# Encoder layer in split fp32: row and block sums of the second MLP product placed elsewhere, and the q and k evictions at the highest priority on VectorE

## The chip, the cores and the metric

One core of one Trainium2 chip. The metric is the device time of one launch in microseconds (us), the median of several runs. A core has five engines that run side by side, each with its own queue of instructions that it takes strictly in order: TensorE (PE in the profile), VectorE (DVE), ScalarE (ACT), GpSimd (POOL) and SyncE (SP), which here computes nothing and issues nearly all transfers between HBM and SBUF. Matrix products land in PSUM, in eight banks of 128 x 512 fp32.

## The reference, cut to what matters

The input is x of 1024 rows (positions) by 1024 columns. All is fp32.

```
h = rmsnorm(x, g_mix);  z = h @ w_in;  q, k, v, ... = split(z)
x = x + concat([gated linear attention(q, k, v, ...), spatial gating(...)]) @ w_out
h = rmsnorm(x, g_mlp)
x = x + square(relu(h @ w1)) @ w2          # w1: 1024 x 4096, w2: 4096 x 1024
out = rmsnorm(x, g_final)                  # x * rsqrt(mean(x*x) + eps) * g
```

## The kernel before, in words

**Precision.** TensorE multiplies rounded values, so each operand tile is split in two: `split` rounds a 128 x 512 tile on ScalarE (the cast, L124) and takes the rest on VectorE (the "lo split", L125). A product then takes three matmuls, hi x hi, hi x lo and lo x hi. Both halves live in tiles named xa, of which there are 16: `put2` takes two for each split operand, so splits can run 8 operands ahead of TensorE, which is two pairs of the passes 1 to 3 below.

**The MLP by blocks.** Both MLP products follow a Strassen-Winograd scheme, with 7 block products instead of 8. The first product (`mlp1`, 16 steps p, one for each pair of hidden tiles) computes h = relu(..)^2 by blocks and stores to HBM (tiles hA, hS) the blocks A11, A12, A22 and the sums S1 to S4 that the second product needs. The norm in front of the MLP is not applied to x2 (the x after attention): its row factor is left out of the hidden values and comes back at the end, where out = (x2 + r2 * y), and r2 = 1 / (mean(x2*x2) + eps) for each row. x2 itself is kept in HBM (x2n, natural order) and read again for this.

**The second product** runs in four passes over the same 16 pairs p:
- pass 1: X += A11.B11, Y += A12.B21. At its end the X banks are copied to U on ScalarE, and C11 = Y + U on VectorE (L566).
- pass 2: X += S1.T1, Y += S2.T2, with T1 = B12 - B11 and T2 = B22 - T1 taken on VectorE (`sub2`, L563). At its end u5 = X (ScalarE), U += Y and u5 += U (VectorE).
- pass 3: Y += A22.T4 first, then X += S3.T3, with T4 = B21 - T2 and T3 = T2 - B11.
- pass 4: X += S4.B22; the last three pairs are done bank by bank, so that the rows of a bank can be finished while the next one runs.

X and Y are four banks each (pf and pg in the profile, which lists a bank by its pool). A pass begins to write a bank as soon as the adds or copies that read it at the end of the pass before are done. One block product of a pair (`product2`) is 12 matmuls, a pair of passes 1 to 3 has 24, a pair of pass 4 has 12.

**Row work.** `row_load` brings a half row block of x2 (128 x 512) into a tile (qk for rows 4 to 7, a part of V for rows 0 to 3) and squares it on ScalarE (L872) for r2; `row_add` (L883) adds r2 times one of the blocks C11, U, u5, X, Y; `sq` squares the sums for the last norm; `finish` applies factor and gain gB: a GpSimd multiply (L921) and a ScalarE scaling (L922) for the left half, one VectorE instruction (L924) for the right half.

**Order.** The order on an engine is fixed when the kernel is built, by a list scheduler that models the engines and prefers instructions of higher priority (`tc.high_priority(offset=..)`; HP and HPE are 400, HP2 is 160). On TensorE the program's order is kept. Loads of the four passes are chained in program order by `load2`; which buffers they rotate through is set by `streams` (hidden blocks) and `raws` (weights). A load waits on SP until its buffer is free, and what stands behind it on SP waits too.

**q and k.** Early in the kernel the projections of q and k are taken out of PSUM by `qk_evac` (a VectorE multiply by the row factor, L296, and a ScalarE copy), while the stages of the attention before them (`st_cum`, L335 to L349; `st_kv`, L404 and L410) use the same engines.

Of the kernel before, what the change touches and what calls it, by code (L numbers as in the profile page):

```python
# [7 lines left out]
F32 = mybir.dt.float32  # L8
# [23 lines left out]
def tile_encoder(  # L32
# [110 lines left out]
    one("pad", [P, 32])  # L143
# [145 lines left out]
    def qk_evac(dst, i):  # L289
        def done(ps, hf):  # L290
            r = R[:, hf * 512 : hf * 512 + 512]
            for j in range(2):
# [3 lines left out]
                nc.vector.tensor_tensor(out=t[own], in0=ps[own], in1=r[own], op=ALU.mult)  # L296
# [340 lines left out]


# [54 lines left out]
    def mlp1(p):  # L693
# [36 lines left out]
        nc.scalar.copy(out=h12, in_=b)  # L730
# [4 lines left out]
        keep("S4", p, s4)  # L735

    mlp1(0)
    x2_natural(order[-1])
    for p in range(1, NPAIR):
        mlp1(p)  # L740
# [3 lines left out]
    streams = [("la", 3)] * 3 + [("qin", 2)] * 2 + [("kin", 2)] * 2 + [("kd", 1)]  # L744
    sn = [0, None]

    def load2(t, src):

        ins = nc.sync.dma_start(out=t, in_=src)
        if sn[1] is not None:  # L750
            tc.add_manual_dep(
                ins.ins,
                sn[1].ins.name,
                mybir.DependencyInfo(mybir.DependencyClass.NoSync, mybir.DependencyReason.DATA),
                reason="load order",
            )
        sn[1] = ins
# [299 lines left out]
```

## Time and profile before

| | |
|---|---|
| median of 3 runs | 1052.75 us (1051.12 to 1054.19) |
| the profiled execution | 1054.3 us, of which 1052.5 from its first to its last instruction |
| busy: PE, DVE, ACT, POOL | 1022.5 (97%), 700.7 (67%), 473.4 (45%), 98.2 (9%) us |
| stages (read from the timeline) | projections and mixers 0 to 316, W_out to 414, first MLP product to 716, pass 1 to 803.0, pass 2 to 895.8, pass 3 to 990.7, pass 4 to 1044.8, tail to 1052.5 |

All times are of the slowest (here the only) core. A busy TensorE is not one at its peak: its share counts a matmul that runs at half clock as busy too. Since TensorE is busy nearly throughout, the time is TensorE's work, plus its waits, plus what its clock loses. "Granted clock" is the share of full speed (2.4 GHz; the other level is 1.2 GHz) that the chip gave TensorE in a stretch.

### The profile page before, as it was taken

The page shows a single profiled execution, that of the slowest core. Times are in us where ns is not written, and L with a number is a line of the kernel's source. Part 1 is how long each engine was busy: PE and PEld are TensorE (multiplying, and loading weights), DVE is VectorE, ACT ScalarE, POOL GpSimd, SP SyncE. Part 2 cuts the span into 40 slices and gives each one's busy share as a digit, 9 for nine tenths or more (in the row PEclk, how much of TensorE's full clock was granted, in tenths as well). Part 3 has the DMA queues.
Part 4 walks back from the last instruction along what each step waited for, and adds up shares of the span by engine and source line. Part 5 has one row for each costly group of instructions (what it writes and reads, how often), then busy time and mean ns, then how long its engine had stood idle before and what let it go on. Part 6 is the DMA issues. An engine that isn't in the chain of part 4 may idle for free. (4 is left out here: it accounts for less than half of the span.)

```text
span 1052.5 us, 14294 instructions
## 1 busy us (share of the span) xinstructions
PE 1022.5 (97%) x5014; PEld 832.1 (79%) x5014; DVE 700.7 (67%) x1172; ACT 473.4 (45%) x903; POOL 98.2 (9%) x116
## 2 busy tenths in 40 slices
PE   9999999999999999999999999999999999899977
PEld 7887778777878888888888888888887887687855
DVE  6247867666664557887776776756457767657784
ACT  7534626455454545433333333334444444345563
POOL 1001423323221000000000000000000000000241
PEclk9999999999999999999999999999999999999989
DMA  9322111111112544554353443339764555464532
GB/s 317 137 76 65 41 51 50 31 31 31 51 40 93 156 124 138 171 183 148 128 184 129 156 171 124 140 140 329 233 208 161 188 171 161 122 198 155 164 112 80
DMA packets 84119, 141.78 MB, mean 135 GB/s; under 512 B 8784, under 2 KB 17744, under 8 KB 84048
## 3 DMA queue, kind: packets, MB, share of 16 engines
q1 hardware_dynamic: 82896, 138.79, 40.2%
q10 hardware_dynamic: 1152, 2.10, 0.5%
q8 instruction: 39, 0.64, 0.2%
q14 instruction: 32, 0.26, 0.1%
HBM read 103.10 MB, written 37.75 MB: 134 GB/s over the span
## 5 line engine op out<-in xcount | busy, mean ns | idle before, releaser
L106 PE MATMUL pg<-xa,xa 128*128 128x512 f32 x768 | 189.5, 397 | 15.4 <-DVE xa L125 9.7
L106 PEld LDWEIGHTS pg<-xa,xa 128*128 128x128 f32 x768 | 145.4, 191 | 51.2 <-DVE xa L125 12.0
L106 PE MATMUL pf<-xa,xa 128*128 128x512 f32 x576 | 139.4, 391 | 0.0
L106 PE MATMUL pf<-xa,wh 128*128 128x512 f32 x336 | 135.9, 405 | 0.0
L106 PE MATMUL pf<-xb,wh 128*128 128x512 f32 x336 | 132.2, 393 | 0.0
L106 PEld LDWEIGHTS pf<-xa,xa 128*128 128x128 f32 x576 | 109.1, 189 | 23.0
L106 PE MATMUL pf<-xa,wl 128*128 128x512 f32 x320 | 125.9, 393 | 0.0
L106 PE MATMUL pf<-V,xa 128*128 128x512 f32 x336 | 91.7, 389 | 0.0
L124 ACT CAST xa<-xb 128x512 fp32r<-128x512 f32 x76 | 47.1, 621 | 98.0 <-PE pf L106 74.7
L125 DVE TENSOR_TENSOR xa<-xb,xa 128x512 fp32r<-128x512 f32 x76 | 52.1, 688 | 55.7 <-ACT xa L124 55.6
L125 DVE TENSOR_TENSOR wl<-wr,wh 128x512 fp32r<-128x512 f32 x63 | 48.9, 776 | 50.3 <-ACT wh L124 50.0
L106 PEld LDWEIGHTS pf<-xa,wh 128*128 128x128 f32 x336 | 63.9, 190 | 14.2 <-issue 1.4
L106 PEld LDWEIGHTS pf<-V,xa 128*128 128x128 f32 x336 | 63.1, 188 | 13.1
L106 PEld LDWEIGHTS pf<-xb,wh 128*128 128x128 f32 x336 | 63.8, 190 | 12.2
L106 PEld LDWEIGHTS pf<-xa,wl 128*128 128x128 f32 x320 | 60.7, 190 | 13.3
L913 POOL TENSOR_SCALAR r<-r 128x1 f32<-128x1 f32 x8 | 3.3, 416 | 680.0 <-ACT tmp L911 679.5
L124 ACT CAST wh<-wr 128x512 fp32r<-128x512 f32 x63 | 38.8, 616 | 60.4 <-PE pf L106 55.1
L124 ACT CAST xa<-k 128x512 fp32r<-128x512 f32 x49 | 30.5, 623 | 78.3 <-PE pf L106 75.5
L106 PE MATMUL pf<-xb,xa 128*128 128x512 f32 x192 | 53.9, 389 | 0.0
L106 PE MATMUL pf<-qk,xa 128*128 128x512 f32 x176 | 52.9, 389 | 0.0
L124 ACT CAST xa<-la 128x512 fp32r<-128x512 f32 x42 | 26.1, 621 | 49.6 <-PE pg L106 30.0
L125 DVE TENSOR_TENSOR xa<-la,xa 128x512 fp32r<-128x512 f32 x42 | 30.0, 713 | 27.4 <-ACT xa L124 27.4
(290 smaller groups left out, 1887.2 us busy)
## 6 DMA issues: line engine op xcount, KB each, us to landing
k<-w SPq DMA_DIRECT2D x64, 256.0 KB, 2.9
hA<-kn SPq DMA_DIRECT2D x32, 256.0 KB, 2.9
hS<-wr SPq DMA_DIRECT2D x32, 256.0 KB, 3.4
la<-hS SPq DMA_DIRECT2D x26, 256.0 KB, 2.7
qk<-xn SPq DMA_DIRECT2D x16, 256.0 KB, 5.4
wr<-wsv SPq DMA_DIRECT2D x16, 256.0 KB, 2.5
wr<-wo SPq DMA_DIRECT2D x16, 256.0 KB, 2.6
x2n<-tmp SPq DMA_DIRECT2D x16, 256.0 KB, 3.9
```

The source lines that it names most:

```text
L106: nc.tensor.matmul(out=o, lhsT=lhsT, rhs=rhs, start=start, stop=stop, skip_group_check=more)
L124: nc.scalar.copy(out=hi, in_=src)
L125: nc.vector.tensor_tensor(out=lo, in0=src, in1=hi.bitcast(F32), op=ALU.subtract)
L913: nc.gpsimd.tensor_scalar(out=r[:, 4:5], in0=r[:, 0:1], scalar1=EPS, scalar2=None, op0=ALU.add)
```

## The change

It consists of these parts.

1. The L296 multiply of `qk_evac` is put at the highest priority.
2. The squares of x2 for r2 leave passes 3 and 4. Eight new loads of a whole row block (128 x 1024, into tile R) and eight ScalarE squares stand in the first MLP product instead, one in each of its steps p = 2 to 9, ordered behind the step's last PSUM copy. r2 follows at p = 10 by two small VectorE instructions.
3. The hidden loads of passes 1 and 2 rotate through 16 buffers instead of 8 (the 8 qk tiles are added), and the weight loads after p = 3 no longer use qk.
4. B11 of pairs 0 and 1 is kept in R from pass 1 on; its two reloads in pass 2 go.
5. `sub2` puts each subtraction behind the lo split that was made 8 operands earlier, so that VectorE no longer reaches a subtraction long before it is needed. The subtractions T3 move with this from pass 2 into pass 3.
6. Additions to rows 4 to 7 move from the end of pass 3 to its pairs 2 to 5, those to rows 0 to 3 from pass 4 to pairs 9 to 12 of pass 3, with their loads; there the left halves of rows 0 to 3 are multiplied by gB as well (VectorE).
7. gB is loaded in pass 3, pair 2, instead of before pass 1.
8. `finish`: for rows 4 to 7 the left half is done by one VectorE instruction (L933 of the kernel after) in place of GpSimd's and ScalarE's, for rows 0 to 3 only ScalarE's scaling is left.

```diff
 def split(src, hi, lo, scale=None):
-            nc.vector.tensor_tensor(out=lo, in0=src, in1=hi.bitcast(F32), op=ALU.subtract)
+            return nc.vector.tensor_tensor(out=lo, in0=src, in1=hi.bitcast(F32), op=ALU.subtract)
 def qk_evac(dst, i):
-                nc.vector.tensor_tensor(out=t[own], in0=ps[own], in1=r[own], op=ALU.mult)
+                with tc.high_priority(offset=HP):
+                    nc.vector.tensor_tensor(out=t[own], in0=ps[own], in1=r[own], op=ALU.mult)
+    def in_order(ins, after):
+        if after is not None:
+            tc.add_manual_dep(ins.ins, after.ins.name, ...NoSync..., reason="order of use")
+        return ins
+    def row_square(t, after):
+        r = sb("R", 1, [P, D])
+        nc.sync.dma_start(out=r, in_=x2n[t])
+        in_order(nc.scalar.activation(out=r, in_=r, func=AF.Square, accum_out=r2[:, t : t + 1]), after)
     for p in range(1, NPAIR):
-        mlp1(p)
+        last = mlp1(p)
+        if 2 <= p < 2 + NT:
+            row_square(p - 2, last)
+        if p == 2 + NT:
+            nc.vector.tensor_scalar(out=r2, in0=r2, scalar1=1.0 / D, scalar2=EPS, op0=ALU.mult, op1=ALU.add)
+            nc.vector.reciprocal(out=r2, in_=r2)
-    streams = [("la", 3)] * 3 + [("qin", 2)] * 2 + [("kin", 2)] * 2 + [("kd", 1)]
+    streams = [("la", 3), ("qin", 2), ("qk", 8), ("kin", 2), ("la", 3), ("qk", 8)] + [("la", 3), ("qin", 2), ("qk", 8), ("kin", 2), ("kd", 1), ("qk", 8)]
 def put2(src):
-            split(src, a, b)
+            loq.append(split(src, a, b))
 def sub2(out, a, b):
-            sub(out, a, b)
+            in_order(nc.vector.tensor_tensor(out=out, in0=a, in1=b, op=ALU.subtract), loq[-8])
     # pass 1
-            raws = [("qk", 8)] * 8 + [("wr", 2), ("tmp", 2), ("sg", 2), ("kn", 2)] * 2
+            raws = [("wr", 2), ("tmp", 2), ("sg", 2), ("kn", 2)] * 2
     # pass 2
-        if p < 2:
-            B11[p] = w2_load(2 * p, 0, big[0][:, p])
     # pass 3
+    streams = [("la", 3), ("qin", 2), ("kin", 2), ("la", 3), ("qin", 2), ("kin", 2), ("la", 3), ("kd", 1)]
-        if p >= 8 and p % 2 == 0:
-            row_load(4 + (p - 8) // 2)
-        if p == NPAIR - 1:
-            row_scale(4)
-            for tt in range(4):
-                row_add(4 + tt, 0, U[tt])
-                row_add(4 + tt, 1, u5[tt])
+        if p == 2:
+            gB = sb("R", 1, [P, D])
+            load2(gB, gfin.broadcast_to([P, D]))
+        if 2 <= p < 6:
+            t = 2 + p
+            row_load(t)
+            row_add(t, 0, U[t - 4])
+            row_add(t, 1, u5[t - 4])
+        if 9 <= p < 13:
+            t = p - 9
+            row_load(t)
+            row_add(t, 0, C11[t])
+            sq(r0[t], 0, rows[t, 0], 512)
+            row_add(t, 1, u5[t])
+            nc.vector.tensor_tensor(out=rows[t, 0], in0=rows[t, 0], in1=gB[:, 0:512], op=ALU.mult)
 def finish(t, r):
-        left_eng.tensor_tensor(out=left, in0=left, in1=gB[:, 0:512], op=ALU.mult)
-        tc.keep_in_program_order(nc.scalar.activation(out=left, in_=left, func=AF.Copy, scale=s))
+        if t < 4:
+            tc.keep_in_program_order(nc.scalar.activation(out=left, in_=left, func=AF.Copy, scale=s))
+        else:
+            nc.vector.scalar_tensor_tensor(out=left, in0=left, scalar=s, in1=gB[:, 0:512], op0=ALU.mult, op1=ALU.mult)
     # pass 4
-        if p % 2 == 0 and p < 8:
-            row_load(p // 2)
-        if p == 8:
-            row_scale(0)
-            for tt in range(4):
-                row_add(tt, 0, C11[tt])
-                sq(r0[tt], 0, rows[tt, 0], 512)
-                row_add(tt, 1, u5[tt])
```

TensorE's order is the same in both kernels. What moves stands on VectorE, ScalarE and SP. Three places on VectorE follow; a row is its number, the line, the operation, output<-inputs with buffer numbers, and the tile's shape. Lines of the kernel after are one to some more than before: L297 answers to L296, L350 to L349, L567 to L566, L799 to L563, L882 to L883.

The first is at the second half of the third attention head (projection of k), before and then after. Here the qk tiles are what `qk_evac` writes, the X tiles the attention's states, kin the keys that TensorE waits for.

```order
211 L341 TENSOR_TENSOR sm_1697<-sm_1697 128x8
212 L296 TENSOR_TENSOR qk_1727<-pf_1593,R_496 64x512
213 L410 SCALAR_TENSOR_TENSOR X_1392<-X_1392,sm_1448 64x128
214 L296 TENSOR_TENSOR qk_1730<-pf_1593,R_496 64x512
215 L346 SCALAR_TENSOR_TENSOR qin_1703<-qin_1703,qk_1159 128x512
216 L125 TENSOR_TENSOR wl_1943<-wr_1940,wh_1942 128x512
217 L410 SCALAR_TENSOR_TENSOR X_1392<-X_1392,sm_1174 64x128
218 L349 TENSOR_TENSOR kin_1702<-kin_1702,qk_1682 128x512
```

```order
209 L342 TENSOR_TENSOR sm_1697<-sm_1697 128x8
210 L411 SCALAR_TENSOR_TENSOR X_1392<-X_1392,sm_1448 64x128
211 L297 TENSOR_TENSOR qk_1727<-pf_1593,R_496 64x512
212 L297 TENSOR_TENSOR qk_1730<-pf_1593,R_496 64x512
213 L411 SCALAR_TENSOR_TENSOR X_1392<-X_1392,sm_1448 64x128
214 L347 SCALAR_TENSOR_TENSOR qin_1703<-qin_1703,qk_1159 128x512
215 L125 TENSOR_TENSOR wl_1943<-wr_1940,wh_1942 128x512
216 L350 TENSOR_TENSOR kin_1702<-kin_1702,qk_1682 128x512
```

The two multiplies stand side by side, and the state update that stood right ahead of kin is gone from there (it follows behind).

The second is the end of pass 2 and the start of pass 3. The adds that read pg are U0 to U3; each must be done before pass 3 writes that bank.

```order
986 L125 TENSOR_TENSOR xa_8116<-V_6575,xa_8115 128x512
987 L125 TENSOR_TENSOR xa_8150<-qin_8143,xa_8149 128x512
988 L566 TENSOR_TENSOR wl_7231<-pg_7255,wl_7231 128x512
989 L563 TENSOR_TENSOR sg_8291<-sg_8291,xb_7472 128x512
990 L566 TENSOR_TENSOR wl_7232<-pg_7256,wl_7232 128x512
991 L125 TENSOR_TENSOR xa_8155<-sg_8147,xa_8154 128x512
992 L566 TENSOR_TENSOR k_7239<-k_7239,wl_7231 128x512
993 L566 TENSOR_TENSOR wl_7233<-pg_7257,wl_7233 128x512
994 L566 TENSOR_TENSOR wh_7234<-pg_7258,wh_7234 128x512
```

```order
972 L799 TENSOR_TENSOR V_6602<-xb_7395,V_6602 128x512
973 L125 TENSOR_TENSOR xa_8175<-kin_8168,xa_8174 128x512
974 L567 TENSOR_TENSOR wl_7258<-pg_7282,wl_7258 128x512
975 L567 TENSOR_TENSOR wl_7259<-pg_7283,wl_7259 128x512
976 L125 TENSOR_TENSOR xa_8180<-sg_8172,xa_8179 128x512
977 L567 TENSOR_TENSOR k_7266<-k_7266,wl_7258 128x512
978 L567 TENSOR_TENSOR wl_7260<-pg_7284,wl_7260 128x512
979 L567 TENSOR_TENSOR k_7267<-k_7267,wl_7259 128x512
980 L567 TENSOR_TENSOR wh_7261<-pg_7285,wh_7261 128x512
```

The subtraction L563 between U0 and U1 (its tile sg is a weight for a pair far ahead) is gone; an add to u5 (tile k) stands between U2 and U3.

The third is pass 4, before and after, from about its middle. V are rows 0 to 3, the qk tiles rows 4 to 7; wh, k are blocks C11 and u5.

```order
1112 L125 TENSOR_TENSOR xa_9164<-xb_7624,xa_9163 128x512
1113 L883 SCALAR_TENSOR_TENSOR V_9000<-wh_7235,r_8085,V_9000 128x512
1114 L883 SCALAR_TENSOR_TENSOR V_9000<-k_7239,r_8085,V_9000 128x512
1115 L883 SCALAR_TENSOR_TENSOR V_9000<-wh_7236,r_8085,V_9000 128x512
1116 L883 SCALAR_TENSOR_TENSOR V_9000<-k_7240,r_8085,V_9000 128x512
1117 L883 SCALAR_TENSOR_TENSOR V_9000<-k_7237,r_8085,V_9000 128x512
1118 L883 SCALAR_TENSOR_TENSOR V_9000<-k_7241,r_8085,V_9000 128x512
1119 L883 SCALAR_TENSOR_TENSOR V_9000<-k_7238,r_8085,V_9000 128x512
1120 L883 SCALAR_TENSOR_TENSOR V_9000<-k_7242,r_8085,V_9000 128x512
1121 L125 TENSOR_TENSOR xa_9182<-la_9179,xa_9181 128x512
```

```order
1107 L125 TENSOR_TENSOR xa_9102<-qin_9099,xa_9101 128x512
1108 L933 SCALAR_TENSOR_TENSOR qk_8266<-qk_8266,r_8953,R_8264 128x512
1109 L937 SCALAR_TENSOR_TENSOR qk_8268<-qk_8268,r_8953,R_8264 128x512
1110 L125 TENSOR_TENSOR xa_9106<-xb_7496,xa_9105 128x512
1111 L933 SCALAR_TENSOR_TENSOR qk_8320<-qk_8320,r_8967,R_8264 128x512
1112 L937 SCALAR_TENSOR_TENSOR qk_8322<-qk_8322,r_8967,R_8264 128x512
1113 L125 TENSOR_TENSOR xa_9124<-kin_9121,xa_9123 128x512
```

The eight additions in a row are gone; the pairs of `finish` instructions stand apart, with a lo split between them.

## Rows read from the trace of the kernel before

**Rows 1.** The page: span, and GB/s in 40 equal slices.

```profile
span 1052.5 us, 14294 instructions
...
GB/s 317 137 76 65 41 51 50 31 31 31 51 40 93 156 124 138 171 183 148 128 184 129 156 171 124 140 140 329 233 208 161 188 171 161 122 198 155 164 112 80
```

**Rows 2.** Windows by stage: length, busy time of each engine, granted clock, DMA share, GB/s.

```profile
414.00:716.00 302.00, 302.00 (x1338) 250.13 (x1338) 221.90 (x347) 108.75 (x193) 0.00 (x0) 1.00 0.46 154
716.00:803.00 87.00, 87.00 (x385) 72.04 (x384) 49.26 (x78) 39.80 (x71) 0.00 (x0) 1.00 0.72 249
803.00:895.80 92.80, 90.16 (x385) 72.47 (x383) 69.50 (x112) 38.55 (x69) 0.00 (x0) 0.98 0.53 170
895.80:990.70 94.90, 89.74 (x385) 73.07 (x385) 62.10 (x101) 41.03 (x80) 0.00 (x0) 0.98 0.53 169
990.70:1044.80 54.10, 46.54 (x193) 36.67 (x192) 39.05 (x56) 32.75 (x78) 20.33 (x27) 0.94 0.23 78
```

**Rows 3.** What PE waited for: us in total, times, longest.

```profile
PE pg L106 <- DVE xa L125: 9.7, 6, 6.6
PE pg L106 <- DVE wl L566: 3.6, 3, 2.0
PE pf L106 <- DVE qk L296: 3.0, 2, 2.6
PE pg L106 <- DVE kin L349: 2.6, 2, 1.3
PE pg L106 <- DVE wh L566: 1.3, 1, 1.3
```

**Rows 4.** Timeline of PE: start, us, what, [idle before <- releaser].

```profile
129.90 0.47 PE L106 MATMUL pf<-wh,xa 128*128 128x512 f32 x1 [2.60 <-DVE qk L296]
...
808.20 0.98 PE L106 MATMUL pg<-xa,xa 128*128 128x512 f32 x3 [1.32 <-DVE wh L566]
...
899.66 0.96 PE L106 MATMUL pg<-xa,xa 128*128 128x512 f32 x3 [1.98 <-DVE wl L566]
...
1021.58 1.65 PE L106 MATMUL pg<-xa,xa 128*128 128x512 f32 x3 [6.61 <-DVE xa L125]
```

**Rows 5.** Window around the end of pass 1, columns as in rows 2.

```profile
789.00:815.00 26.00, 24.42 (x98) 18.90 (x97) 20.27 (x33) 11.14 (x20) 0.00 (x0) 0.93 0.47 156
```

**Rows 6.** Timeline of DVE at the start of pass 2.

```profile
805.18 0.68 DVE L566 TENSOR_TENSOR wh<-pg,wl 128x512 f32<-128x512 f32 x1
806.85 0.69 DVE L563 TENSOR_TENSOR qk<-qk,V 128x512 f32<-128x512 f32 x1 [0.99 <-DMA qk<-w]
807.46 0.68 DVE L566 TENSOR_TENSOR wh<-pg,wl 128x512 f32<-128x512 f32 x1
```

**Rows 7.** Timeline of DVE at the start of pass 3.

```profile
898.31 0.69 DVE L563 TENSOR_TENSOR sg<-sg,xb 128x512 f32<-128x512 f32 x1 [1.72 <-DMA sg<-w]
```

**Rows 8.** Timeline of SP at the end of pass 2.

```profile
895.19 0.42 SPq L749 DMA_DIRECT2D sg<-w  x1
```

**Rows 9.** Timeline of DVE, third attention head.

```profile
188.21 1.02 DVE L410 SCALAR_TENSOR_TENSOR X<-X,sm 64x128 f32<-64x128 f32 x1
```

**Rows 10.** What ACT waited for from 716 to 1045, as in rows 3.

```profile
ACT tmp L872 <- DMA qk<-x2n: 13.6, 4, 4.8
```

**Rows 11.** Timeline of DVE in pass 4.

```profile
1013.15 0.74 DVE L883 SCALAR_TENSOR_TENSOR V<-wh,r,V 128x512 f32<-128x512 f32 x1
1013.81 5.44 DVE L883 SCALAR_TENSOR_TENSOR V<-k,r,V 128x512 f32<-128x512 f32 x5
1019.17 1.75 DVE L125 TENSOR_TENSOR xa<-la,xa 128x512 fp32r<-128x512 f32 x1
```

**Rows 12.** Timeline of POOL in pass 4.

```profile
1016.39 1.64 POOL L921 TENSOR_TENSOR V<-V,R 128x512 f32<-128x512 f32 x1
```

**Rows 13.** Timeline of SP ahead of pass 1.

```profile
711.17 0.32 SPq L749 DMA_DIRECT2D qin<-hA  x1
```

**Rows 14.** Timeline of ACT ahead of pass 1.

```profile
713.85 0.62 ACT L124 CAST xa<-qin 128x512 fp32r<-128x512 f32 x1 [2.54 <-DMA qin<-hA]
```

More of the change, by code (lines that the diff above doesn't have):

```diff
@@ L142, in tile_encoder @@
     ccols = one("cols", [P, 24])
-    one("pad", [P, 32])
+    one("pad", [P, 16])
     warm = sb("tmp", 2)
@@ L636, in tile_encoder @@
             x2_natural(order[n - 1])
+    def in_order(ins, after):
+        if after is not None:
+            tc.add_manual_dep(
+                ins.ins,
+                after.ins.name,
+                mybir.DependencyInfo(mybir.DependencyClass.NoSync, mybir.DependencyReason.DATA),
+                reason="order of use",
+            )
+        return ins
     NPAIR = NFF // 2
@@ L729, in mlp1 @@
         h12 = sb("kn", 2)
-        nc.scalar.copy(out=h12, in_=b)
+        last = nc.scalar.copy(out=h12, in_=b)
         relu2(h12, h12)
@@ L735, in mlp1 @@
         keep("S4", p, s4)
+        return last
+    r2 = one("r2", [P, 8])
+    def row_square(t, after):
+        r = sb("R", 1, [P, D])
+        nc.sync.dma_start(out=r, in_=x2n[t])
+        in_order(nc.scalar.activation(out=r, in_=r, func=AF.Square, accum_out=r2[:, t : t + 1]), after)
     mlp1(0)
@@ L739, in tile_encoder @@
     for p in range(1, NPAIR):
-        mlp1(p)
+        last = mlp1(p)
[4 more added lines that the diff above has]
+            nc.vector.reciprocal(out=r2, in_=r2)
     HP2 = 160
-    streams = [("la", 3)] * 3 + [("qin", 2)] * 2 + [("kin", 2)] * 2 + [("kd", 1)]
-    sn = [0, None]
+    streams = [("la", 3), ("qin", 2), ("qk", 8), ("kin", 2), ("la", 3), ("qk", 8)] + [("la", 3), ("qin", 2), ("qk", 8), ("kin", 2), ("kd", 1), ("qk", 8)]
+    loq = [None]
+    sn = [None]
     def load2(t, src):
[L749 to L757, printed above, removed]
+        sn[0] = in_order(nc.sync.dma_start(out=t, in_=src), sn[0])
         return t
@@ L867, in row_load @@
         for dh in range(2):
-            r = sb("qk", 8) if t >= 4 else rows0[0][:, 2 * t + dh]
-            rows[t, dh] = r
-            load2(r, x2n[t, :, dh * 512 : dh * 512 + 512])
-            junk = sb("tmp", 2, [P, 512], BF16)
-            nc.scalar.activation(out=junk, in_=r, func=AF.Square, accum_out=ss2[:, 8 * dh + t : 8 * dh + t + 1])
-    def row_scale(t0):
-        c = slice(t0, t0 + 4)
-        c2 = slice(8 + t0, 12 + t0)
-        nc.vector.tensor_tensor(out=r2[:, c], in0=ss2[:, c], in1=ss2[:, c2], op=ALU.add)
-        nc.vector.tensor_scalar(out=r2[:, c], in0=r2[:, c], scalar1=1.0 / D, scalar2=EPS, op0=ALU.mult, op1=ALU.add)
-        nc.vector.reciprocal(out=r2[:, c], in_=r2[:, c])
+            rows[t, dh] = sb("qk", 8) if t >= 4 else rows0[0][:, 2 * t + dh]
+            load2(rows[t, dh], x2n[t, :, dh * 512 : dh * 512 + 512])
     def row_add(t, dh, src, sl=slice(0, 512)):
@@ L885, in row_add, with sq @@
         )
+    def sq(r, i, src, n):
+        junk = sb("tmp", 2)
+        nc.scalar.activation(out=junk[:, :n], in_=src, func=AF.Square, scale=D**-0.5, accum_out=r[:, i : i + 1])
+        if i == 0:
+            nc.gpsimd.tensor_scalar(out=r[:, 4:5], in0=r[:, 0:1], scalar1=EPS, scalar2=None, op0=ALU.add)
+        else:
+            nc.gpsimd.tensor_tensor(out=r[:, 4:5], in0=r[:, 4:5], in1=r[:, i : i + 1], op=ALU.add)
     X, Y = [pf() for _ in range(4)], [pg() for _ in range(4)]
     raws = [("wr", 2), ("sg", 2), ("kn", 2)] * 2
+    streams = [("la", 3), ("qin", 2), ("kin", 2), ("la", 3), ("qin", 2), ("kin", 2), ("la", 3), ("kd", 1)]
+    r0 = [sb("r3", 8, [P, 8]) for _ in range(4)]
     for p in range(NPAIR):
@@ L937, in tile_encoder @@
         row_add(t, 1, X[tt])
-        r = sb("r3", 4, [P, 8])
+        r = sb("r3", 8, [P, 8])
         sq(r, 0, rows[t, 0], 512)
         sq(r, 1, rows[t, 1], 512)
-        finish(t, r, nc.gpsimd)
+        finish(t, r)
     X = [pg() for _ in range(4)]
@@ L946, in tile_encoder @@
     tail = []
-    r0 = [sb("r3", 4, [P, 8]) for _ in range(4)]
     for p in range(NPAIR):
@@ L971, in tile_encoder @@
             sq(r0[tt], i + 1, rows[tt, 1][:, c0 : c0 + n], n)
-        finish(tt, r0[tt], nc.gpsimd if tt < 3 else nc.vector)
+        finish(tt, r0[tt])
 def _constants():
```

34 lines of the change are left out of this document (12 added, 22 removed).

## The prediction

> **What bounds the kernel now.** I read the busy shares first: TensorE is busy 97% of the span [rows 1], so only what it waits, and what its clock loses, can be won. The windows by stage say where that is [rows 2]. Pass 1 is the yardstick: 87.0 us with TensorE never idle and the clock at 1.00, so 5.44 us for a pair and 2.72 us for a block product. Pass 2 has the same matmuls and takes 92.8: 5.8 lost. Pass 3 takes 94.9: 7.9 lost. Pass 4 has half of them, 43.5, and takes 54.1: 10.6 lost. The sum is 24.3 us. The first MLP product loses nothing (302.00 of 302.00 busy).
>
> The waits of TensorE give the causes [rows 3]. Of 24.3 us, 14.6 are waits for VectorE with a name: 9.7 for lo splits (L125), 3.6 and 1.3 for the adds that free banks (L566). Much of the rest is the clock: 0.98, 0.98 and 0.94 granted in passes 2, 3 and 4 make 0.02 x 92.8 + 0.02 x 94.9 + 0.06 x 54.1 = 7.0 us. The clock falls around the waits: 0.93 in the 26 us that hold the wait of 1.32 at 808.20, 1.00 in the whole of pass 1 before [rows 2, 4, 5]. So a wait that goes takes its share of the clock's loss with it, and I count a pass by its length. Ahead of the passes, TensorE waits 3.0 us for the q and k multiplies and 2.6 for kin.
>
> The timeline of VectorE shows why it is late though it is busy only two thirds of passes 2 and 3 [rows 2]: its queue is in order, and a subtraction that waits for its weight stops all behind it. At 806.85 a subtraction has waited 0.99 us for a load, and the add that frees a bank starts only at 807.46, 0.61 later (the step from one instruction to the next) [rows 6]. At 898.31 the same costs 1.72, for a load that SP issued at 895.19 only [rows 7, 8].
>
> **The change part by part.**
>
> *q and k.* The two multiplies stand next to each other, so one state update (L410) less lies ahead of the second, and one less ahead of kin. The one ahead of kin took 1.02 us [rows 9], so about 1.0 goes there. At 129.90 [rows 4] an update of the same shape is passed; bounds are nothing and 1.02, and since 1.02 is long for a 64 x 128 tile (a 128 x 512 tile steps on after 0.61), I take 0.4. Sum 1.4. The end above is the whole 5.6 of rows 3 and some clock.
>
> *Squares into the first MLP product.* Eight squares of 128 x 1024; a ScalarE pass over 128 x 512 takes 0.62 [rows 14], so some 1.3 each, 10 in all. ScalarE is busy 108.75 of 302 there [rows 2], 7 us of each 18.9 us step, and the squares stand behind the step's last copy, so they lie in idle time. The eight loads of 512 KB fit a stretch at 154 GB/s. Cost nothing; without the cover 1.3 each, 10 at most. They take 16 squares off ScalarE in passes 3 and 4, and the waits for x2n: 13.6 us in 4 waits, up to 4.8 each [rows 10], in which every cast behind stood still too.
>
> *Start of pass 1.* R is now used up to the end of the first product, and the loads of pair 0 (but one) stand behind a load that waits on SP until TensorE frees its buffer. Before, the first load like that was issued at 711.17 and its cast ran at 713.85, 2.7 later [rows 13, 14]. Now B11 comes one place behind, so its cast ends near 714.9, its lo split near 715.6, and pass 1 wants it at 716.0. Bounds: nothing, and 2.0 if the loads behind share the bandwidth. I take 0.4 lost.
>
> *Start of pass 2 and its middle.* The subtractions no longer run ahead to weights that are in flight, and with 16 buffers the hidden loads run further ahead. The four C11 adds then follow each other with only splits between, at 0.61 each from 803.0, and pass 2 wants their banks from 805.7 (one product later) on, one each 0.68 us: the last is done near 805.2. The lo splits of pass 2 have 7 VectorE instructions for a pair before and 6 after (T3 moved), 3.7 of 5.44 us. I take the whole 5.8 as won; the bound below is nothing.
>
> *Start of pass 3.* Bank i of Y is complete 2.04 - 0.68 i us before the pass ends, and pass 3 wants bank i at 0.68 i after it. From the order after, with steps of 0.61, U0 is done at -0.76, U1 at -0.16, then a split and an add to u5, U2 at 1.65 (wanted 1.36), another u5 add, U3 at 2.85 (wanted 2.04 + 0.3). Some 0.8 stays, say 1.0. Before, waits of 0.99 to 1.98 each stood here [rows 4, 7].
>
> *Within pass 3.* 6 instructions of 0.61 for a pair, 3.7 us. Pairs 2 to 5 have two additions more, which step by 0.66 [rows 11]: 5.0 of 5.44. Pairs 9 to 12 have two additions and a gB multiply: 5.6, so VectorE falls behind by 0.15 a pair, 0.6 in all. Splits have three products, 8.2 us, from the freeing of their tile to their use, less 1.3 for the cast and the split itself: cover enough. The additions wait for loads of x2n; those are issued with loads for the next pairs and come 2 to 3 us ahead of use as I lay them out. So pass 3 keeps 1.0 and gives 6.9.
>
> *Pass 4.* Before, eight additions stand in a row: three at 0.66 and five in 5.44, then a split of 1.75, and TensorE waits 6.61 at 1021.58 [rows 4, 11]. The row sums of five and the split are 3.2 us over their uncontended price (5 x 0.66 + 0.61 = 3.9 against 7.1); three GpSimd multiplies of 1.64 lie beside them [rows 12]. After, additions and GpSimd multiplies are both gone: VectorE has 32 splits and 20 other instructions, 32.7 of 43.5 us, at most six others in a row, 4.0 us, against a look-ahead of four pairs, 10.9 us. The tightest place that I find has 1.2 us left, at the fifth and sixth pair; I leave 1.2 of the 10.6 lost, and take 9.4. Below: nothing won.
>
> *finish, tail.* The tail is bank by bank as before, 7.7 us.
>
> **The sum.** 1.4 - 0.4 + 5.8 + 6.9 + 9.4 = 23.1 us. The profiled execution took 1054.3, so 1031.2 for such a one; it lies 1.55 above the median of the runs shown, 1052.75, and I forecast 1029.7.
>
> **A rule against part of it.** The traces tie the clock's loss to the waits (0.93 beside a wait of 1.32 us) [rows 4, 5]. The Trainium skill, "TensorE: Matmul & The Clock Gate", section on HAM oscillation, has the clock fall when TensorE stands idle for long, as in waits for each tile's load; by it waits as short as these would not be the cause. The trace disagrees, and I go by the trace. If the clock's loss has another cause and stays, the result is that of the second rival below.
>
> **Rivals.**
>
> 1. *Late transfers at the start of pass 3.* gB's load holds SP until R is free (the split of pair 1's B11), and then loads of x2n, weights and hidden blocks for three pairs come in a burst. At the 329 GB/s that the busiest slice reached [rows 1] 256 KB takes 0.8 us and all come in time. At half of that, as in most slices of passes 2 to 4, some 14 loads take 0.8 us more each, 11 us; the look-ahead does not cover it: 1040.7. For it: the 4.8 us waits for x2n. Against: pass 1 moves 249 GB/s without a wait [rows 2].
>
> 2. *Only the waits go.* The clock falls as before and small gaps stay. Of the waits of 14.6 in the passes, 1.0 + 1.2 stay, so 12.4 + 1.4 - 0.4 = 13.4: 1039.4. A like time results if the waits at the two pass ends stay (3.6 + 1.3 and their share of the clock's loss), because subtractions still meet late loads. Against: loads stand three pairs ahead.
>
> 3. *More.* With the multiplies early, the clock no longer falls in the heads: rows 3's 5.6 go entire instead of 1.4. With some 1.0 less kept in passes 3 and 4: about 1024.5.
>
> 4. *Slower.* The eight rows' additions stand in VectorE's queue ahead of splits, and each waits for its x2n load as ScalarE's squares did, in the place of the waits removed. Before, such a wait stopped ScalarE; now it stops VectorE, which has no room to catch up in pairs 9 to 12. The look-ahead forgives about 6 us once in each group of four. Eight waits of 4.8 [rows 10] less 12 make 26.4, more than the 23.1 won: 1056. It decides from 4.4 us a wait. Against: the loads are chained two pairs ahead, and their buffers (qk) are free by then.
>
> 5. *Nothing happens*: another wait of equal size takes over behind those removed, as VectorE's total work stays; 1052. Against: pass 1, with as many loads, has none.
>
> **Chances.** Forecast 0.62 (1027 to 1034), rival 1 0.13, rival 2 0.11, rival 3 0.06, rival 4 0.04, rival 5 0.04. A measurement here can tell 0.3%, about 3 us, from no change: faster 0.92, same 0.04, slower 0.04. The range reaches to the cases on both sides: below to half way to rival 3 with its bounds, 1025; above to rivals 1 and 2, 1041. Rivals 4, 5 and the far halves of the others are left out.
>
> **What would show it.** Right: passes of about 87, 88 and 45 us with clock at 1.00; no subtraction waiting for a weight around the pass ends; no wait of TensorE above 1 us after 803. At the heads, waits of 2.2 and 0.3 where 2.60 and 1.3 stood. Wrong: SP idle behind gB's load and splits late around pairs 2 to 6 of pass 3; additions that wait for x2n; a wait at the start of pass 1 above 2 us; granted clock below 1.00 without a wait.

## The result, and the profile after

The changed kernel takes 1024.75 us (median of 4 runs, 1024.36 to 1024.87), the kernel before 1052.32 beside it: a ratio of 0.9736 (0.9719 to 0.9753). The forecast was 1029.7, from 1025 to 1041: the gain is larger than foretold, and just outside the range. The profiled execution took 1024.64, 29.7 less than the one before, where the sum said 23.1.

The windows by stage of the changed kernel answer to [rows 2]; the first row is the stretch up to W_out, the last four are the passes, each from its first matmul on (columns as there).

```profile
0.00:309.00 309.00, 304.14 (x1875) 241.68 (x1876) 199.53 (x394) 161.01 (x327) 73.03 (x82) 1.00 0.24 79
...
407.00:708.71 301.71, 301.71 (x1337) 249.89 (x1335) 219.49 (x344) 115.88 (x206) 0.00 (x0) 1.00 0.48 165
708.71:796.44 87.73, 87.64 (x385) 71.92 (x384) 51.36 (x82) 40.92 (x74) 0.00 (x0) 1.00 0.79 280
796.44:883.48 87.04, 87.04 (x385) 72.07 (x384) 62.96 (x101) 38.56 (x69) 0.00 (x0) 1.00 0.43 136
883.48:971.51 88.03, 87.64 (x386) 71.92 (x385) 74.83 (x121) 39.22 (x73) 13.07 (x4) 1.00 0.59 200
971.51:1015.19 43.68, 43.68 (x193) 35.85 (x191) 30.66 (x48) 23.00 (x50) 10.45 (x16) 1.00 0.30 97
```

The passes take 87.7, 87.0, 88.0 and 43.7 where they took 87.0, 92.8, 94.9 and 54.1. That is 22.3 won (306.5 after 328.8): 0.7 lost at the start of pass 1, then 5.8, 6.9 and 10.4 won. The prediction said 21.7 (-0.4 + 5.8 + 6.9 + 9.4). The rest, 7.3, lies ahead of pass 1: it begins at 708.7 where it began at 716.0. There the prediction had 1.4. The first MLP product, which has taken in the eight squares, is no longer than before (301.7 after 302.0).

What TensorE waits for in the changed kernel, beside [rows 3]:

```profile
PE pf L106 <- DVE qk L297: 1.9, 2, 1.5
PE pg L106 <- DVE kin L350: 1.3, 1, 1.3
PE pg L106 <- POOL tmp L147: 1.3, 1, 1.3
PE pg L106 <- DVE wh L567: 0.2, 1, 0.2
PE pg L106 <- DVE V L479: 0.2, 1, 0.2
PE pg L106 <- DVE wl L567: 0.2, 1, 0.2
```

In the passes 0.4 us is left of 14.6. In the heads of the attention 3.2 is left of 5.6: the waits explain 2.4 of the 7.3, not more. The other 5 is the clock: 1.00 up to 309 us, where three half-speed stretches of 3.4 us stood before, each worth 1.7. The same stretch of the kernel before (columns as in [rows 2]):

```profile
0.00:316.00 316.00, 309.05 (x1874) 245.94 (x1875) 201.14 (x393) 160.71 (x327) 72.88 (x82) 0.98 0.24 77
```

The start of pass 3 on VectorE went as laid out from the order, steps of 0.61 included (timeline):

```profile
882.03 1.28 DVE L567 TENSOR_TENSOR wl<-pg,wl 128x512 f32<-128x512 f32 x2
883.23 0.68 DVE L125 TENSOR_TENSOR xa<-sg,xa 128x512 fp32r<-128x512 f32 x1
883.83 0.68 DVE L567 TENSOR_TENSOR k<-k,wl 128x512 f32<-128x512 f32 x1
884.43 0.68 DVE L567 TENSOR_TENSOR wl<-pg,wl 128x512 f32<-128x512 f32 x1
885.03 0.68 DVE L567 TENSOR_TENSOR k<-k,wl 128x512 f32<-128x512 f32 x1
885.63 0.68 DVE L567 TENSOR_TENSOR wh<-pg,wh 128x512 f32<-128x512 f32 x1
```

U0 and U1 end at 883.3, U2 at 885.1, U3 at 886.3; no subtraction stands between them that waits for a load. TensorE waits 0.16 and 0.22 for the last two.

### The profile page after: what moved, and what is told of

The parts are those of the page before. It is cut to its first block, busy times and chain, and to the rows that moved or that the text cites. A ratio compares the mean times of both kernels' runs of the same rounds, so it can differ in the third digit from the quotient of the medians.

```text
span 1022.8 us, 14249 instructions
## 1 busy us (share of the span) xinstructions
PE 1009.8 (99%) x5014; PEld 825.1 (81%) x5014; DVE 696.6 (68%) x1175; ACT 470.3 (46%) x883; POOL 101.4 (10%) x109
## 4 chain that ended last, share of the span: by engine, by line
PE 93%; DVE 4%; ACT 1%; issue 1%; POOL 0%; DMA 0%; POOLq 0%; SPq 0%; ACTq 0%
PE pf L106 63%; PE pg L106 28%; PE pg L110 1%; DVE X L411 1%; DVE qk L297 1%; DVE X L405 1%; ACT X L401 0%; DMA R<-w 0%; DVE kin L350 0%; DVE kin L341 0%; DVE sg L487 0%; DVE wl L567 0%; DVE xa L125 0%; DVE qin L347 0%; DVE wl L125 0%
## 5 line engine op out<-in xcount | busy, mean ns | idle before, releaser
L106 PE MATMUL pg<-xa,xa 128*128 128x512 f32 x768 | 182.5, 389 | 0.4 <-DVE wh L567 0.2
L890 POOL TENSOR_SCALAR r<-r 128x1 f32<-128x1 f32 x8 | 14.6, 1820 | 647.1 <-ACT tmp L888 646.9
L124 ACT CAST xa<-la 128x512 fp32r<-128x512 f32 x34 | 21.2, 623 | 46.0 <-PE pf L106 25.9
L106 PEld LDWEIGHTS pf<-xb,xa 128*128 128x128 f32 x192 | 36.0, 188 | 7.5
```

Source lines behind the costliest of these rows:

```text
L106: nc.tensor.matmul(out=o, lhsT=lhsT, rhs=rhs, start=start, stop=stop, skip_group_check=more)
L890: nc.gpsimd.tensor_scalar(out=r[:, 4:5], in0=r[:, 0:1], scalar1=EPS, scalar2=None, op0=ALU.add)
```

## The experiments

Three questions: what made 7.3 us ahead of pass 1; which part frees the passes; what made the wait of 6.61 in pass 4.

### Both kernels again

Unchanged copies of the kernel before and of the changed one.

> The kernel before, unchanged, to see how much of its time is the same from run to run. If a fall of TensorE's clock belongs to the wait beside it (theory A), each run has the mean clock of 0.987 of the profile shown, the same six falls of some 3.4 us at half clock, and times within 1 us of 1052.3. If the clock falls at some waits and not at others from one run to the next (theory B), the runs differ by 1.7 us for each fall, the mean clocks by 0.0016 each, and a second profile has its falls at other waits than 129.90, 190.00, 244.62, 808.20, 899.66 and 1021.58.

Measured: 1055.48 (1051.5 to 1059.75, 12 runs), mean clocks of 0.985 to 0.990. The second profile falls to half speed at 129.9, 191.3 and 245.9 as the first, but not at 808 any more, where TensorE waits 1.48 us, and newly at 973.0. Theory B.

> The changed kernel, unchanged, beside the kernel before on one chip. Theory B (TensorE's clock falls at short waits in some runs and not in others): its runs agree within 1 us, since few waits are left at which it could fall, while those of the kernel before spread over 8 us. If the gain was partly luck of the first four runs: some runs lie 3 to 5 us above 1024.75, with falls at the waits of 1.50 and 1.32 in the heads.

Measured: 1024.69 (1024.43 to 1025.06), ratio 0.9749 (0.9733 to 0.9765); no fall before the tail. With few waits, the time repeats within 0.7 us over eight runs; the kernel before spread from 1048.3 to 1059.75 over all that ran.

### Part 1 alone, and all but part 1

```diff
-                nc.vector.tensor_tensor(out=t[own], in0=ps[own], in1=r[own], op=ALU.mult)
+                with tc.high_priority(offset=HP):
+                    nc.vector.tensor_tensor(out=t[own], in0=ps[own], in1=r[own], op=ALU.mult)
```

> The kernel before with part 1 alone (the two multiplies of the q and k evictions at the highest priority). Its VectorE order in the heads is that of the changed kernel. Theory A (the 7.3 us that the stretch ahead of pass 1 won are all of part 1: 2.4 us of waits and three falls of the clock): 1052.3 - 7.3 = 1045.0, clock 1.00 up to 316 us. Theory B (the clock's part is not tied to this change): 2.4 us less, 1049.9, with a clock below 1.00 somewhere in the heads. If the prediction's own term had been right: 1.4 less, 1050.9.

> The changed kernel without part 1. Theory A: 1024.75 + 7.3 = 1032.0, with waits of 2.6, 1.3 and 1.3 in the heads and three falls of the clock there, and the four passes as in the changed kernel (306.5 us). Theory B: 1027.2 plus 1.7 for each fall that happens to come. If parts 1 and the rest help each other: another sum than 1052.3 - 1045.0.

Measured: part 1 alone 1049.32, ratio 0.994 (0.9918 to 0.9962), 4 to 9 us less; all but part 1 1030.09 (1027.3 to 1031.6), 5.3 more than the changed kernel. So part 1 is worth some 5: 2.4 in waits, which are the same in each profile, and a share of clock that is not. The medians are those of theory B (1049.9, and 1027.2 with one or two falls) and not of theory A (1045.0 and 1032.0), except that the fall which B wanted in the heads of part 1 alone did not come in its profile. The profile of part 1 alone has no fall in the heads, that of all but part 1 has three (and takes 1031.5, near the upper end).

The sharpest rows are of a run made for another purpose (part 5 alone, below), whose heads are in the old order. Its waits there, and the window that holds them, columns as in [rows 2]:

```profile
PE pf L106 <- DVE qk L296: 3.0, 2, 2.6
PE pg L106 <- DVE kin L349: 2.6, 2, 1.3
```

```profile
120.00:260.00 140.00, 134.76 (x966) 106.29 (x965) 103.66 (x213) 70.34 (x147) 45.59 (x49) 1.00 0.13 38
```

And the same window of the second profile of the kernel before, with the same waits (3.0 and 2.6):

```profile
120.00:260.00 140.00, 134.82 (x928) 106.54 (x928) 102.30 (x208) 68.54 (x139) 44.66 (x47) 0.96 0.13 37
```

Same instructions, same waits, clock 1.00 in one and 0.96 in the other, and 38 matmuls more on record in the same 140 us (966 against 928). A short wait makes a fall possible, not certain. In the old order three such waits (2.6, 1.3, 1.3) were followed by 10 falls in five profiles, of 15 possible; in the new order the two that are left (1.5, 1.3) by 2 in fourteen, of 28. The falls of the old order come together: the five profiles have three, three, three, one and none, so the fifteen are not fifteen independent cases, and the two profiles of the kernel before are both among those with three.

### The order of the subtractions (part 5) and the buffers (part 3)

Part 5 taken from the changed kernel; part 3 taken from it; and each put alone into the kernel before.

```diff
 # sub_free
-            in_order(nc.vector.tensor_tensor(out=out, in0=a, in1=b, op=ALU.subtract), loq[-8])
+            sub(out, a, b)
 # old_streams (and its reverse, streams_only)
-    streams = [("la", 3), ("qin", 2), ("qk", 8), ("kin", 2), ...]
-            raws = [("wr", 2), ("tmp", 2), ("sg", 2), ("kn", 2)] * 2
+    streams = [("la", 3)] * 3 + [("qin", 2)] * 2 + [("kin", 2)] * 2 + [("kd", 1)]
+            raws = [("qk", 8)] * 8 + [("wr", 2), ("tmp", 2), ("sg", 2), ("kn", 2)] * 2
```

> The changed kernel without part 5: the subtractions of weights keep their priority, but no longer stand behind the lo split made 8 operands before, so they run ahead on VectorE again. If the order of the subtractions is what freed the ends of passes 1 and 2 (the prediction's step): waits of 1 to 3 us for the bank adds come back at both, with some clock, so 6 to 10 us more, 1031 to 1035. If the loads that run further ahead (part 3: 16 buffers) suffice by themselves: within 1.5 us of 1024.75.

Measured: 1026.56 (1025.98 to 1026.83), 1.8 more. Only the wait at the end of pass 1 is back (timeline of TensorE), the others stay away:

```profile
800.42 0.97 PE L106 MATMUL pg<-xa,xa 128*128 128x512 f32 x3 [1.14 <-DVE wh L567]
```

> The changed kernel with the buffers of the hidden and weight loads as before (part 3 undone). Theory C (what frees VectorE in passes 2 and 3 is that loads run further ahead; the order of the subtractions, undone in the run before, was worth 1.8 us only): lo splits and bank adds wait again for late loads, 0.7 + 0.3 in pass 2 and 1 to 3.6 at its end, and with some clock 4 to 9 us more, 1029 to 1034. Theory D (the order of the subtractions and the buffers each suffice alone): within 1.5 us of 1024.75.

Measured: 1025.05 (1024.29 to 1026.29). Without the buffers nothing is lost.

> The kernel before with part 3 alone (16 buffers for the hidden loads, weights without qk). Theory C: the waits of VectorE for weights fall to some 5 us from some 39, the waits of TensorE in pass 2 (0.74, 0.32) and at its end (3.6 in three) go, the one at the end of pass 1 (1.5) stays: 6 to 9 us less than the kernel before. Theory D': the buffers alone do nothing, since the subtractions still run as far ahead as loads come: within 2 us of the kernel before.

Measured: 1048.08, ratio 0.9949 (0.9922 to 0.9976), 2.5 to 8 us less, between the two theories. TensorE's waits in pass 2 are gone and those for bank adds at its end are shorter; by the timeline passes 2 and 3 take 90.7 and 93.7, 3.3 less together, and the profile has one fall of the clock in the heads where the kernel before had three. But VectorE still waits for weights, 37 us in all against 42 (the three largest, from pass 1 to 4):

```profile
DVE wr L563 <- DMA wr<-w: 11.7, 8, 2.3
DVE sg L563 <- DMA sg<-w: 9.5, 7, 2.1
DVE kn L563 <- DMA kn<-w: 7.1, 6, 1.7
```

> The kernel before with part 5 alone (each subtraction behind the lo split made 8 operands before). Theory C: the wait at the end of pass 1 (1.5, and its share of the clock) goes, those in pass 2 and at its end become smaller but stay where loads are late: 2 to 4 us less. The prediction's step (the order of the subtractions frees both ends): 1.5 + 3.6 us of waits and two falls of 1.7 us, 8 less.

Measured: 1039.61 (1037.6 to 1041.8), ratio 0.9898 (0.9875 to 0.992): 8 to 13 us from a handful of lines. In its profile passes 2 and 3 alone give 11.7 (columns as in [rows 2], which has 92.8 and 94.9):

```profile
797.74:884.78 87.04, 87.04 (x385) 72.07 (x384) 62.87 (x101) 38.54 (x69) 0.00 (x0) 1.00 0.57 179
884.78:973.78 89.00, 87.96 (x386) 71.86 (x384) 68.02 (x112) 41.10 (x81) 0.00 (x0) 1.00 0.55 174
```

In the passes VectorE waits for no weight at all. TensorE keeps 7.0 us of waits for splits, of which 6.6 is the one in pass 4; the one in pass 3 (1.6 to 2.1 before) is gone too, and of the bank adds 1.0 is left:

```profile
PE pg L106 <- DVE xa L125: 7.0, 3, 6.6
...
PE pg L106 <- DVE wl L566: 0.8, 1, 0.8
...
PE pg L106 <- DVE wh L566: 0.2, 1, 0.2
```

So the prediction's step holds: the order of the subtractions frees both ends (one wait of 0.8 stays), and theory C falls. But why does its removal from the changed kernel cost 1.8 only? One run more, without parts 3 and 5 together.

> The changed kernel without parts 3 and 5 together. Each alone cost 0.3 and 1.8 us. If the wider buffers are what hid the late loads where the order of the subtractions was taken away: the waits of VectorE for weights come back whole, and those of TensorE in pass 2 and at its end with them, 1031 to 1036. If other parts (the row work that left VectorE and ScalarE, the two loads less) hide them: 1026 to 1028, with the wait of 1.1 at the end of pass 1 alone.

Measured: 1031.23 (1027.6 to 1033.8), 6.5 more, where each alone cost 0.3 and 1.8: the buffers are a cover for subtractions that run ahead, and it is not needed as long as these stand in their place. VectorE waits for weights again, 26 us. The profile is of the fastest of the four, 2.9 above the changed kernel; what made the other three slower was not seen. It has waits of pass 2 back, 1.9 in three, and not those at the ends of passes 1 and 2. The two largest:

```profile
855.34 2.81 PE L106 MATMUL pg<-xa,xa 128*128 128x512 f32 x11 [1.14 <-DVE xa L125]
...
867.56 2.79 PE L106 MATMUL pg<-xa,xa 128*128 128x512 f32 x11 [0.53 <-DVE xa L125]
```

So the rest of what part 5 is worth in the kernel before seems to be covered by other parts of the change; by which was not tried.

### Pass 4

The additions to rows 0 to 3 put back in one row (A), with GpSimd's multiplies for rows 0 to 2 beside them, and GpSimd's finish for all rows alone (P):

```diff
 # pile (A): out of pass 3, into pass 4, ahead of the splits of pair 9
...
+        if p == 8:
+            last = loq[-1]
+            for tt in range(4):
+                last = in_order(row_add(tt, 0, C11[tt]), last)
+                sq(r0[tt], 0, rows[tt, 0], 512)
+                last = in_order(row_add(tt, 1, u5[tt]), last)
...
 # pool_back (P): in finish, for all t
+        left_eng = nc.vector if t == 3 else nc.gpsimd
+        left_eng.tensor_tensor(out=left, in0=left, in1=gB[:, 0:512], op=ALU.mult)
+        tc.keep_in_program_order(nc.scalar.activation(out=left, in_=left, func=AF.Copy, scale=s))
```

> The changed kernel with the eight additions to rows 0 to 3 put back into pass 4 in one row on VectorE behind the splits of pair 8, the gB multiplies of these rows following on VectorE; loads, squares for r2 and GpSimd's part stay as changed. The prediction's account (eight additions of 0.66 are 5.3 us, against a look-ahead of four pairs, 10.9): no wait of TensorE in pass 4, within 1 us of 1024.75. Theory F (the row of additions alone makes the wait, since the look-ahead is not full there): a wait of some 4 us (6.6 less the 2.6 to 3.2 us that the row took beyond its uncontended price) and some clock, 1029 to 1031.

> As the run before with the row of eight additions in pass 4, and with the gB multiplies of rows 0 to 2 on GpSimd beside them, as in the kernel before. The eight additions should take about 7.4 us instead of 5.3, and single ones 1 us or more, as in the kernel before. Theory G (GpSimd's contention makes the wait): none or a small wait without it, and 3 to 6.6 us with it, 1029 to 1034. If additions and GpSimd together still leave no wait: what made it in the kernel before was that the look-ahead had been used up by the squares of x2 on ScalarE.

> The changed kernel with the finish of the left halves as before (GpSimd multiply by gB, ScalarE scaling for all rows; part 8 undone, additions early). From the order: GpSimd's multiplies fall beside splits and the finish of rows 4 to 7 at the start of pass 4. The prediction counted about 1 us of VectorE time for each multiply that overlaps, four of them, all inside the look-ahead: within 1 us of 1024.75, the tail up to 1 us longer if rows 0 to 3 wait for GpSimd.

Measured, in this order: 1025.4, 1026.0 and 1024.9, all within 1.3 us. The row of eight (timeline of VectorE, run A) is there and runs at 0.66 a step:

```profile
990.38 0.75 DVE L882 SCALAR_TENSOR_TENSOR V<-wh,r,V 128x512 f32<-128x512 f32 x1
...
992.37 3.40 DVE L882 SCALAR_TENSOR_TENSOR V<-k,r,V 128x512 f32<-128x512 f32 x5
```

TensorE waits 0.36 for it. So the row alone is not the cause, and theory F falls. It is near the limit, though. By its place in the order the row stands ahead of the splits of pair 9. It begins 18.6 us into the pass, and TensorE wants the last of these splits near 24.9 (it waits up to 25.2): some 6 us of look-ahead for a row of 5.3 and two splits.

The second run does not test theory G, since GpSimd does not run beside the row in it. Its first multiply begins at 1002.31, long behind the row, and the five additions take 3.40 again (timelines of VectorE and GpSimd):

```profile
992.12 3.40 DVE L882 SCALAR_TENSOR_TENSOR V<-k,r,V 128x512 f32<-128x512 f32 x5
```

```profile
991.90 10.32 POOL L890 TENSOR_SCALAR r<-r 128x1 f32<-128x1 f32 x1 [6.74 <-ACT tmp L888]
1002.31 1.29 POOL L926 TENSOR_TENSOR V<-V,R 128x512 f32<-128x512 f32 x1
```

GpSimd stands in a 128 x 1 instruction for 10.32 us there, where the same one takes 0.56 in A + P below; why was not tried. So it stayed open whether the cause is the row beside GpSimd's multiplies, the squares of x2 on ScalarE, or the state in which pass 4 begins. Four runs more, with the squares put back as well (S); where S and A are both back, so are the loads of these rows in pass 4:

```diff
 # S, in pass 4
+        if p % 2 == 0 and p < 8:
+            for dh in range(2):
+                junk = sb("tmp", 2, [P, 512], BF16)
+                nc.scalar.activation(out=junk, in_=rows[p // 2, dh], func=AF.Square, accum_out=r0[p // 2][:, 6 + dh : 7 + dh])
```

> The changed kernel with pass 4 as in the kernel before in three things: S, eight ScalarE squares of x2 rows 0 to 3 (their sums unused here; r2 still comes from the first MLP product), A, the row of eight additions behind pair 8, and P, the finish with GpSimd's multiplies and ScalarE's scaling for all rows. If pass 4's loss of 10.6 us is made within pass 4: it comes back, a wait of 4 to 6.6 us near 40 us before the end, 1031 to 1036. If no wait comes back, the loss was carried into pass 4 from pass 3 (splits that were not ahead when it began): within 1.5 us of 1024.75.

> S and A without P (finish as changed). Theory H (ScalarE's queue is what uses up the look-ahead, by the squares of x2 and by scalings that wait for GpSimd, and the row of additions then bites): with P gone, ScalarE has 4 scalings less and no wait for GpSimd, so the wait is half of that with all three, 2 to 3 us: 1026 to 1029. Theory F (additions): 1025.4 as without S.

> S and P without A (additions early; S squares the rows as they then are, sums unused). Theory H: ScalarE is late as with all three, but VectorE has no row of additions, so the casts' delay alone shows: short waits of 0.2 to 0.6 for casts, 1025 to 1027. If P and S are enough for the whole wait: 1031 to 1036.

> A and P (for all rows) without S. Theory H: without the squares ScalarE keeps up: under 1.5 us more than 1024.75. Theory G (GpSimd's part, for rows 4 to 7 too, makes the wait): 1029 to 1034.

Measured, medians of four runs each, beside 1024.7 of the changed kernel, with what the profiles show of pass 4: its length, how far into it the row of additions begins, what the last five additions take, and the longest wait of TensorE (us):

| put back into pass 4 | time | more | pass 4 | row begins | five additions | longest wait |
|---|---|---|---|---|---|---|
| nothing | 1024.7 | | 43.7 | | | none |
| A (additions) | 1025.4 | 0.7 | 44.3 | 18.6 | 3.40 | 0.36 |
| A, GpSimd for rows 0 to 2 | 1026.0 | 1.3 | 44.4 | 18.6 | 3.40 | 0.36 |
| P (finish by GpSimd and ScalarE) | 1024.9 | 0.2 | 43.8 | | | none |
| S + A | 1026.0 | 1.3 | 44.3 | 18.6 | 3.39 | 0.35 |
| S + P | 1029.4 | 4.6 | 46.9 | | | 2.17 |
| A + P | 1030.6 | 5.8 | 49.1 | 18.6 | 5.48 | 3.52 |
| S + A + P | 1035.4 | 10.7 | 52.6 | 22.1 | 5.45 | 5.10 |
| the kernel before | 1052.3 | | 54.1 | 21.1 | 5.44 | 6.61 |

All three together bring back 8.9 of the 10.4 us in pass 4. The profiled execution loses 2 us more ahead of pass 4, with a fall of the clock in the heads, and that of S + P has such a fall too. The changed kernel itself was not run beside these, so differences of 1 us say little.

With P each of the others costs 4 to 6, without P 0.7 and 0.6. Theory H foretold neither A + P (under 1.5 more) nor S + P (1025 to 1027); theory G had A + P right (1029 to 1034). P acts in two places.

*Beside VectorE.* In A + P the row begins 18.6 us into pass 4 as in A, so ScalarE has not held it up. But GpSimd's multiplies now lie beside it (timelines of VectorE and TensorE):

```profile
992.73 5.48 DVE L882 SCALAR_TENSOR_TENSOR V<-k,r,V 128x512 f32<-128x512 f32 x5
998.13 1.76 DVE L125 TENSOR_TENSOR xa<-qin,xa 128x512 fp32r<-128x512 f32 x1
```

```profile
1000.54 11.63 PE L106 MATMUL pg<-xa,xa 128*128 128x512 f32 x43 [3.52 <-DVE xa L125]
```

The five additions and the split behind take 5.48 and 1.76 where they took 3.40 and 0.69 in A, 3.15 more, and TensorE's wait is 3.16 longer, 3.52 after 0.36. A fall of the clock behind the wait is worth 1.7 more. This is what the prediction had named, at the price that it had read (3.2). In S + P, without the row, a finish and two splits beside three multiplies take 1.77, 1.76 and 1.75 where they take 0.75, 0.69 and 0.69 alone, and TensorE waits 2.17 for the last.

*In ScalarE's queue*, but only with S as well: S + A begins its row at 18.6 too. The timeline of ScalarE with all three shows how:

```profile
983.71 0.73 ACT L925 ACTIVATE qk<-qk,r 128x512 f32<-128x512 f32 x1 [0.62 <-POOL r L920]
...
986.18 0.61 ACT L124 CAST xa<-la 128x512 fp32r<-128x512 f32 x1
988.20 0.73 ACT L925 ACTIVATE qk<-qk,r 128x512 f32<-128x512 f32 x1 [1.41 <-POOL r L920]
...
990.06 0.60 ACT L124 CAST xa<-xb 128x512 fp32r<-128x512 f32 x1
```

Between two casts lie 3.9 us: a scaling that waits 1.41 for GpSimd's factor, then two squares. TensorE needs two casts in 2.72. At 990.72 it waits for a cast for the first time: the look-ahead is used up. Only then comes the row of additions (timeline of VectorE), 3.5 us later than in A and A + P, five of them in 5.45 as in [rows 11], and behind it the wait of TensorE:

```profile
997.99 5.45 DVE L882 SCALAR_TENSOR_TENSOR V<-k,r,V 128x512 f32<-128x512 f32 x5
1003.36 1.75 DVE L125 TENSOR_TENSOR xa<-qin,xa 128x512 fp32r<-128x512 f32 x1
```

```profile
1005.77 2.50 PE L106 MATMUL pg<-xa,xa 128*128 128x512 f32 x5 [5.10 <-DVE xa L125]
```

The kernel before has the same two things ahead of its wait: a scaling that waits 1.56, a first wait for a cast at 1007.74, and a row that begins 21.1 us into the pass (timelines of ScalarE, TensorE and VectorE, before):

```profile
1005.22 0.73 ACT L922 ACTIVATE qk<-qk,r 128x512 f32<-128x512 f32 x1 [1.56 <-POOL r L918]
```

```profile
1007.74 0.50 PE L106 MATMUL pg<-xa,xa 128*128 128x512 f32 x1 [0.51 <-ACT xa L124]
```

```profile
1011.82 0.74 DVE L883 SCALAR_TENSOR_TENSOR V<-wh,r,V 128x512 f32<-128x512 f32 x1
```

Five additions take 5.45 beside GpSimd's multiplies and 3.40 without them, and the split behind, beside the third multiply, 1.75 after 0.69: 3.1 for the three. The Trainium skill, "SBUF — State Buffer", section on who interferes with whom, has a VectorE instruction with two SBUF inputs and a GpSimd one that reads SBUF shut each other out. The rows agree with that.

### A try at the waits that are left

```diff
 # kin_first: in st_cum and at the end of mlp1
+        with tc.high_priority(offset=HP):
             nc.vector.scalar_tensor_tensor(out=qi, in0=qi, scalar=0.125, in1=q2[h, hf], op0=ALU.mult, op1=ALU.mult)
             nc.vector.tensor_tensor(out=ki, in0=ki, in1=k2[h, hf], op=ALU.mult)
...
+        with tc.high_priority(offset=HP):
+            last = nc.scalar.copy(out=h12, in_=b)
```

> The changed kernel with two more instructions kinds at the highest priority: the q and k multiplies of the attention stage (L347, L350 of the changed kernel) and the ScalarE copy that ends a step of the first MLP product (whose delay cost TensorE 0.8 us at the start of pass 1 in one profile). If the waits that are left in the heads (1.50 and 1.32) come from instructions placed ahead of them: 1 to 2.8 us less, 1022 to 1023.7. If they come from ScalarE's exponentials and table loads: no change, within 0.5 of 1024.75.

Measured: 1025.15 (1024.67 to 1025.18), no change; the waits of 1.5 and 1.3 stay. But VectorE's order is the same as without the edit from its first instruction to its last, so what another order would give at these waits is not shown.

## Why the prediction was too cautious, step by step

- **q and k: the term that failed.** The prediction counted one state update less ahead of each of two waits, 0.4 and 1.0. It had 1.4 for this term; the profiled pair shows 7.3. Measured: 2.60 became 1.50 and 1.3 went altogether, 2.4, and with them went falls of the clock that the sum left out here (5.1 in the profiled pair, some 3 on average, since part 1 is worth about 5 by the medians). Why the clock falls at such a wait in one execution and not in another stays open. The mechanism was right, the size was not. In the passes the prediction had counted the clock with the waits, by taking each pass by its length; in the heads it took the waits alone. The profile had what it needed: the stretch that holds these waits has a clock of 0.98. Rival 3, at 1024.5 and 0.06, had the condition right (the clock no longer falls in the heads) and deserved far more. Its price was not this one: it had all 5.6 of the waits go, where 2.4 of them and some 3 of clock went, so that its time fits is partly luck.
- **Which execution the sum started from.** The profiled execution before had three falls in the heads; two of the other four with the same order there had one and none. The sum made against it holds for that one, and a range around it must hold the spread of the clock.
- **Start of pass 1:** 0.4 expected, 0.7 lost in the first profile, of which the named waits are under 0.1; single waits of 0.2 to 0.8 in others. Within its bounds.
- **Passes 2 and 3:** 12.7 expected, 12.7 won, and 11.7 by part 5 alone; 1.0 left in pass 3 as said. The C11 adds do not have only splits between them in the new order: a subtraction stands there too, but its weight had come.
- **Pass 4:** 9.4 expected, 10.4 won. The contention that the prediction named is there at its price: 3.15 for A + P, 3.2 read. It is not the whole. The prediction missed what made the row late: squares, and scalings that waited in ScalarE's queue for GpSimd, together 3.5 us in S + A + P. The squares were counted as moved at no cost, not as a gain here. And the row of eight had some 6 us of look-ahead in its place, not the 10.9 that four pairs make, so that little was needed beside it.
- **The rule weighed:** the Trainium skill, "TensorE: Matmul & The Clock Gate", section on HAM oscillation, has the clock fall after long idle stretches. Here it fell after 12 of 43 waits of 1.3 to 2.6 us in the heads, so the measurement decides: short waits can do it.
- **Rivals:** the additions did wait for x2n once, 1.7 us of the 4.4 for each of eight that rival 4 needed; the burst of loads in pass 3 came (200 GB/s over the pass, where [rows 2] has 169) and TensorE waited for bank adds only, 0.4 in all.

## What to carry to other kernels

In a kernel whose TensorE is nearly always busy, count a stage by its length against a clean one, everywhere: a short wait can cost as much again in clock, in some runs and not in others. An instruction that waits for a transfer in an in-order queue stops all behind it; tie it to the place of its use, and more buffers may not be needed. When a wait ends in a crowded row on one engine, price the row with what runs beside it, and look back to where the look-ahead was lost: here another engine's queue, waiting for a third. When a run puts something back, see in its trace that the two things really meet: here GpSimd's multiplies once came only behind the row that they were put back to disturb.

## What the runs showed that was not expected

The same wait (1.32 us at kin) in the same surroundings was followed by half a clock for 3.4 us in one execution and by none in another. Why the falls became rarer in the new order (2 of 28 against 10 of 15) than the shorter waits suggest stays open. And parts of a change can cost almost nothing apart and much together: S + A and P cost 1.3 and 0.2, the three 10.7.
